# A hybrid pooling, gating and ConvFFN step, rewritten as one pass over all tokens with a list-scheduled instruction order

## Chip, cores, metric

One Trainium2 chip, all eight NeuronCores. Each core takes one of the eight prompts (2048 tokens, 16 tiles of 128) and an eighth of the samples (128 tokens, one tile), and runs all four layers by itself. The metric is device time in microseconds of the slowest core. A program on all eight cores has a second, slower state in some of its executions, in which the cores of one die (sometimes of both) have a lower granted TensorE clock: 0.808 to 0.816 on die 0 and 0.891 to 0.911 on die 1 in one of the kernel before (3957 us). Each run is marked fast or slow, and only fast runs are compared.

## The reference, cut to what matters

```python
def layer(x, ...):
    z = rmsnorm(x, norm1_g) @ w_in                     # 1024 -> 1536
    p, u, v = z[..., :512], gelu(z[..., 512:1024]), rmsnorm(gelu(z[..., 1024:]), v_norm_g)
    a = pool_mixer(p, pool_past, ...)                  # trailing mean minus token, 4 maps of 128x128, scale
    s = spatial_gate(u, v, w_spatial, b_spatial)       # u * (causal 128x128 W_s @ v + b)
    x = x + concatenate([a, s]) @ w_out                # 1024 -> 1024
    h = rmsnorm(x, norm2_g)
    g = h @ w_gate                                     # 1024 -> 2816
    conv = conv_b + sum(conv_w[k] * shifted(g, k) for k in range(3))
    return x + (gelu(conv) * (h @ w_up)) @ w_down, ...
```

A prompt starts with empty pasts; a sample tile starts from 15 past pooling rows and 2 past gate rows for each sequence. The last rows of both kinds are outputs too.

## The kernel before

It makes two passes ("halves") of all four layers: 8 prompt tiles and the sample tile, then the other 8 prompt tiles. Each pass reads all weights. The FFN goes in groups of 2 chunks of 128 columns. No scheduler reorders it: each engine gets its instructions in the order in which the program names them.

```python
halves = [([8 prompt tiles] + [sample tile], [("p", [0,1,2,3]), ("p", [4,5,6,7]), ("s", [8])]),
          ([8 prompt tiles],                 [("p", [0,1,2,3]), ("p", [4,5,6,7])])]
for half, (tiles, subtiles) in enumerate(halves):
    for l in range(L):
        mixer_phase(half, l, tiles)                 # tile by tile, software-pipelined by hand
        ...
        ffn_phase(half, l, subtiles, hook)
# ... in ffn_phase, for each group of G = 2 chunks, each set of tiles, each chunk:
pg.op("pe", gu, ...)                                # gate and up, 8 + 8 matmuls of 512 columns
if is_s:                                            # sample tile: state in and out by PE transposes
    e.transpose(ps[ga][:, 256:288], scs[csi][:, ci * 128:(ci + 1) * 128], identf[0:32, 0:32])
    # ... later: ACT copies the tail out, PE transposes it, ACT copies it to cso
if want_cs:                                         # last set of the second half: 2 rows, element by element
    pg.dma("sp", ..., [(ncp_o[l][:, c * 128:(c + 1) * 128].rearrange("r p -> p r"), gst[:, 512:514])], slow=True)
# ... down projection of the group, then
pg.op("dve", lambda e: e.tensor_tensor(out=xs[:, slot, :], in0=psall[...], in1=xs[:, slot, :], op=ALU.add))
# cuts: tables, norms, pooling bands, pool map (4 matmuls and 4 scalings a tile), state outputs
```

## Time and profile before

| | before |
|---|---|
| time, median of 20 runs | 3760.6 us (3691.3 to 3899.8) |
| profiled execution, slowest core | 3724.7 us |
| TensorE busy, and standing still | 2902 us, 823 us |
| mean granted clock, that core | 0.930 |
| VectorE, ScalarE, GpSimd busy | 2209, 1349, 465 us |

TensorE (PE) is the fullest engine, and still it stands still for a fifth of the span. "Busy" for matmuls is the time in which at least one was in flight; the granted clock has to be read beside it, since where it is recorded as 0.5 the 512-column matmuls start every 0.43 us (at 317 us of this trace) in place of 0.215 (at 600 us, clock 1.0). PSUM is `psall` in the lines; all 16736 matmuls of this trace write it. The lines themselves are in the prediction.

### The profile page before, as it was taken

The page shows a single profiled execution, that of the slowest core. Times are in us where ns is not written, and L with a number is a line of the kernel's source. Part 1 is how long each engine was busy: PE and PEld are TensorE (multiplying, and loading weights), DVE is VectorE, ACT ScalarE, POOL GpSimd, SP SyncE. Part 2 cuts the span into 40 slices and gives each one's busy share as a digit, 9 for nine tenths or more (in the row PEclk, how much of TensorE's full clock was granted, in tenths as well). Part 3 has the DMA queues.
Part 4 walks back from the last instruction along what each step waited for, and adds up shares of the span by engine and source line. Part 5 has one row for each costly group of instructions (what it writes and reads, how often), then busy time and mean ns, then how long its engine had stood idle before and what let it go on. Part 6 is the DMA issues. An engine that isn't in the chain of part 4 may idle for free.

```text
span 3724.7 us, 50015 instructions; the slowest of 8 cores (3643.9 to 3724.7 us)
## 1 busy us (share of the span) xinstructions
PE 2901.6 (78%) x16736; PEld 1424.5 (38%) x16736; DVE 2209.0 (59%) x2839; ACT 1348.5 (36%) x2883; POOL 465.4 (12%) x851
## 2 busy tenths in 40 slices
PE   0778887788887888878884768887687766887887
PEld 0434444444343444534432423353233422344333
DVE  0457775577745777457773456755475445664667
ACT  0433334333343333533343423353233422344333
POOL 1210002100021000210002210021000200011000
PEclk9999999999999999999997989998798988999998
DMA  9043230432304332043323399708986199940983
GB/s 182 13 94 66 54 58 14 100 67 54 59 13 100 67 57 56 12 95 66 63 45 119 38 86 79 64 9 82 81 57 50 9 85 69 63 47 7 60 60 79
DMA packets 105794, 230.92 MB, mean 62 GB/s; under 512 B 34700, under 2 KB 40012, under 8 KB 105480
## 3 DMA queue, kind: packets, MB, share of 16 engines
q0 software_dynamic: 58832, 183.20, 43.0%
q1 hardware_dynamic: 46712, 44.53, 5.6%
q8 instruction: 140, 2.29, 0.3%
q14 instruction: 110, 0.90, 0.1%
HBM read 398.19 MB, written 13.58 MB: 111 GB/s over the span
## 4 chain that ended last, share of the span: by engine, by line
PE 33%; DMA 22%; DVE 22%; issue 11%; ACT 8%; SPq 2%; another core or an unknown queue 1%; POOL 1%; DVEq 1%; ACTq 0%; POOLq 0%
DMA ncp<-sb_S 15%; DVE sb_xs L719 8%; PE psall L619 7%; PE psall L622 6%; DMA sb_wsl<-wgu_h 4%; PE psall L541 4%; DVE sb_S L686 3%; PE psall L542 3%; DVE sb_S L683 3%; PE psall L713 3%; PE psall L715 3%; PE psall L429 3%; DVE sb_H L516 2%; PE psall L430 2%; ACT sb_S L696 2%
## 5 line engine op out<-in xcount | busy, mean ns | idle before, releaser
L719 DVE TENSOR_TENSOR sb_xs<-psall,sb_xs 128x1024 f32<-128x1024 f32 x748 | 883.3, 1218 | 241.5 <-PE psall L715 236.0
L619 PE MATMUL psall<-sb_h2T,sb_wsl 128*128 128x512 bf16 (+1 forms) x3520 | 768.6, 364 | 292.2 <-DVE sb_H L698 168.2
L622 PE MATMUL psall<-sb_h2T,sb_wsl 128*128 128x512 bf16 (+1 forms) x3520 | 740.4, 355 | 0.0
L696 ACT ACTIVATE sb_S<-sb_S 128x512 f32<-128x512 f32 (+1 forms) x440 | 248.8, 565 | 1141.3 <-DVE sb_S L686 970.1
L713 PE MATMUL psall<-sb_wdl,sb_H 128*128 128x512 bf16 x1496 | 588.1, 393 | 32.3 <-DVE sb_xs L719 28.0
L715 PE MATMUL psall<-sb_wdl,sb_H 128*128 128x512 bf16 x1496 | 587.3, 393 | 0.0
L619 PEld LDWEIGHTS psall<-sb_h2T,sb_wsl 128*128 128x128 bf16 x3520 | 315.8, 101 | 680.7 <-issue 411.6
L698 DVE TENSOR_TENSOR sb_H<-sb_S,psall 128x512 bf16<-128x512 f32 (+1 forms) x440 | 267.4, 608 | 348.8 <-ACT sb_S L696 317.0
L622 PEld LDWEIGHTS psall<-sb_h2T,sb_wsl 128*128 128x128 bf16 x3520 | 329.9, 101 | 350.0 <-issue 31.8
L683 DVE SCALAR_TENSOR_TENSOR sb_S<-sb_S,sb_cw 128x512 f32<-128x512 f32 x352 | 262.3, 745 | 234.0 <-ACT sb_S L680 230.9
L108 POOL DMA_DIRECT2D sb_wsl<-wgu_h x176 | 94.7, 543 | 2227.2 <-PE psall L622 2196.1
L669 ACT ACTIVATE sb_S<-psall 128x512 f32<-128x512 f32 x352 | 207.7, 590 | 407.1 <-PE psall L622 239.4
L686 DVE SCALAR_TENSOR_TENSOR sb_S<-sb_S,sb_cw 128x512 f32<-128x512 f32 x352 | 264.4, 751 | 38.4 <-DVE sb_S L683 2.3
L680 ACT ACTIVATE sb_S<-psall,sb_cb,sb_cw 128x512 f32<-128x512 f32 x352 | 268.0, 761 | 0.0
L541 PE MATMUL psall<-sb_wo,sb_H 128*128 128x512 bf16 x544 | 217.1, 399 | 56.2 <-DVE sb_H L516 50.0
L407 PE MATMUL psall<-sb_identb,sb_H 128*128 128x128 bf16 x1088 | 83.9, 232 | 226.5 <-DVE sb_H L400 226.5
L340 POOL TENSOR_TENSOR sb_stats<-sb_stats,sb_cconst 128x1 f32<-128x1 f32 x221 | 122.8, 556 | 963.9 <-ACT sb_JK L337 679.2
L713 PEld LDWEIGHTS psall<-sb_wdl,sb_H 128*128 128x128 bf16 x1496 | 150.5, 101 | 230.7 <-issue 84.8
L429 PE MATMUL psall<-sb_wi,sb_H 128*128 128x512 bf16 x544 | 217.1, 399 | 17.7 <-ACT sb_JK L337 11.4
L545 DVE TENSOR_TENSOR sb_xs<-psall,sb_xs 128x1024 f32<-128x1024 f32 x68 | 83.3, 1225 | 233.0 <-PE psall L542 225.9
L542 PE MATMUL psall<-sb_wo,sb_H 128*128 128x512 bf16 x544 | 216.6, 398 | 0.0
L430 PE MATMUL psall<-sb_wi,sb_H 128*128 128x512 bf16 x544 | 216.5, 398 | 0.0
(91 smaller groups left out, 2519.1 us busy)
## 6 DMA issues: line engine op xcount, KB each, us to landing
sb_wsl<-wgu_h POOLq DMA_DIRECT2D x176, 512.0 KB, 9.8
sb_wdl<-wd_h POOLq DMA_DIRECT2D x88, 512.0 KB, 13.7
sb_wi<-wi_h POOLq DMA_DIRECT2D x64, 384.0 KB, 17.2
sb_wo<-wo_h POOLq DMA_DIRECT2D x64, 256.0 KB, 24.8
sb_xs<-x_all SPq DMA_DIRECT2D x17, 512.0 KB, 26.1
y_all<-sb_S SPq DMA_DIRECT2D x34, 256.0 KB, 2.6
sb_g1bc<-g SPq DMA_DIRECT2D x8, 512.0 KB, 4.8
sb_g2bc<-g SPq DMA_DIRECT2D x8, 512.0 KB, 12.6
```

The costliest lines, as they stand in the source:

```text
L429: e.matmul(ps[1][:], lhsT=hT[:, k, :], rhs=wi[:, k, 0:512], start=(k == 0), stop=(k == KD - 1))
L430: ins = e.matmul(ps[2][:], lhsT=hT[:, k, :], rhs=wi[:, k, 1024:1536], start=(k == 0), stop=(k == KD - 1))
L541: e.matmul(ps[4][:], lhsT=mixT[:, k, :], rhs=wo[:, k, 0:512], start=(k == 0), stop=(k == KD - 1))
L542: ins = e.matmul(ps[5][:], lhsT=mixT[:, k, :], rhs=wo[:, k, 512:1024], start=(k == 0), stop=(k == KD - 1))
L619: e.matmul(ps[ga][:, 0:ntok], lhsT=wg_[:, k, ci * 128:(ci + 1) * 128], rhs=h2T[:, k, col0:col0 + ntok], start=(k == 0), stop=(k == KD - 1))
L622: ins = e.matmul(ps[gb][:, uo:uo + ntok], lhsT=wu_[:, k, ci * 128:(ci + 1) * 128], rhs=h2T[:, k, col0:col0 + ntok], start=(k == 0), stop=( ...
L683: pg.op("dve", lambda e, acc=acc, gst=gst, w1=w1: e.scalar_tensor_tensor(out=acc[:, 0:512], in0=gst[:, 1:513], scalar=w1, in1=acc[:, 0:512 ...
L686: pg.op("dve", lambda e, acc=acc, gst=gst, w0=w0: e.scalar_tensor_tensor(out=acc[:, 0:512], in0=gst[:, 0:512], scalar=w0, in1=acc[:, 0:512 ...
L696: pg.op("act", lambda e, acc=acc, ge=ge, ntok=ntok: e.activation(out=ge[:, 0:ntok], in_=acc[:, 0:ntok], func=AF.Gelu), reads=[accB], write ...
L713: e.matmul(ps[ya][:], lhsT=hh[:, ci, li * 128:(li + 1) * 128], rhs=wd_[:, ci, 0:512], start=(ci == 0), stop=(ci == gn - 1))
L715: ins = e.matmul(ps[yb][:], lhsT=hh[:, ci, li * 128:(li + 1) * 128], rhs=wd_[:, ci, 512:1024], start=(ci == 0), stop=(ci == gn - 1))
L719: pg.op("dve", lambda e, slot=slot, ya=ya: e.tensor_tensor(out=xs[:, slot, :], in0=psall[:, ya * 512:(ya + 2) * 512], in1=xs[:, slot, :], ...
```

## The change

One pass: all 17 tiles' residual (17 x 4 KB a partition) stays in SBUF, and every weight is read once. Each layer is a first sweep (input projection, pooling bands, spatial gate), a fold of the pool map into the first half of w_out, a second sweep (output projection, residual, norm, transpose) and an FFN in groups of 4 or 3 chunks. States are laid out so that they need no transposes and are stored in one transfer. The program builds a graph of operations with modelled durations, and a list scheduler sets the order on each engine.

```diff
-G = 2
+GROUPS = [4, 4, 4, 4, 3, 3]
...
+    def schedule(self):                 # earliest start first; among the ready, lowest program index
+        ...
+            if avail[e]:
+                o = ops[heapq.heappop(avail[e])]
+            else:
+                o = ops[heapq.heappop(wait[e])[1]]
...
+        xs = SB("xs", (128, NT, D), F32)             # NT = 17
+        wsl = [SB(f"w{i}", (128, 3072), BF16) for i in range(NSLOT)]     # 9 slots, one ring for all weights
...
+        def fold_pool(l):
+            for g in range(4):
+                    e.matmul(ps[b], lhsT=pw[:, g, :], rhs=wov(l, g, 0, 512), start=True, stop=True)
+                    ...
+                pg.op("act", ..., out=wov(l, g, 0, 1024), in_=psall[:, b * 512:(b + 2) * 512])
...
+                    if smp:                          # first sweep, sample tile, after the last use of w_in
+                        for i in range(4):
+                            used("wi", l, i)         # sends the loads that take over these slots
+                    ...
+                        spast = tmp[:, 2 * BLK:3 * BLK].bitcast(BF16)[:, 0:1024]...
+                        pg.dma("pool", "spast", [(spast[0:120], sp_d[l].rearrange("(a r) c -> r a c", a=2))], ...)
...
+            sets = [(list(range(4 * i, 4 * i + 4)), False) for i in range(4)] + [([SMP], True)]
+                        pg.op("pool", 0.4, lambda e: e.tensor_copy(out=halo, in_=src), ...)   # conv rows, was on ACT
...
+        for l in range(L):
+            sweep1(l)
+            fold_pool(l)
+            sweep2(l)
+            ...
+            ffn(l)
+        pg.schedule()
+        pg.emit()
```

## The prediction

> **What bounds the kernel now.** I read the page's engine totals first, then the granted clock of all cores, the table of waits of TensorE, the groups by line and form, the DMA issues, and the order of instructions around single gaps.
>
> ```profile
> span 3724.7 us, 50015 instructions; the slowest of 8 cores (3643.9 to 3724.7 us)
> PE 2901.6 (78%) x16736; PEld 1424.5 (38%) x16736; DVE 2209.0 (59%) x2839; ACT 1348.5 (36%) x2883; POOL 465.4 (12%) x851
> core 1: 3724.7 us, clock 0.930
> ```
>
> No other engine is near full, so TensorE sets the end, but badly: it stands still for 3725 - 2902 = 823 us and its mean granted clock is 0.93. What would it need if it never waited? The order of instructions gives the pace at full clock: successive 512-column matmuls of line 541 and 542 start at 599.90, 600.12 and 600.34, so 0.215 us each (the 0.38 us printed is a pipelined duration); a run of 32 128-column ones of line 464 takes 1.95 us, 0.056 us each. By form the kernel has 10800 of 512 columns (4 x 1408 gate and up, 2 x 1496 down, 4 x 544 projections) and 5760 of 128, plus 176 small fp32 transposes (some 35 us): 2322 + 323 + 35 = 2680 us. The rest of the 2902 busy us, some 220, is lost clock (2680 / 0.93 = 2882). The order around 315 us shows how it is lost:
>
> ```profile
> 314.89 0.27 PE L663 MATMUL psall<-sb_identf_s,sb_csl 128*32 128x128 f32 x1 [2.01 <-ACT sb_csl L660]
> ...
> 316.90 0.63 PE L713 MATMUL psall<-sb_wdl,sb_H 128*128 128x512 bf16 x1
> ...
> 318.61 0.45 PE L713 MATMUL psall<-sb_wdl,sb_H 128*128 128x512 bf16 x1
> 318.90 0.38 PE L715 MATMUL psall<-sb_wdl,sb_H 128*128 128x512 bf16 x1
> ```
>
> After a gap of 2.0 us the same matmul shows 0.63 us instead of 0.38, at half the pace, until full clock is back.[...] The waits name the gaps:
>
> ```profile
> PE psall L407 <- DVE sb_H L400: 226.5, 24, 98.7
> PE psall L619 <- DVE sb_H L698: 168.2, 70, 27.3
> PE psall L619 <- DMA sb_wsl<-wgu_h: 121.7, 13, 17.4
> PE psall L663 <- ACT sb_csl L660: 104.4, 63, 2.4
> ACT sb_S L669 <- DMA ncp<-sb_S: 167.6, 30, 28.6
> ```
>
> The columns are total, times, longest. (a) 98.7 us: the start, in which sixteen projection pieces, three FFN groups, tables and x come in before the first matmul. (b) The chain 669 to 698 waits on the transfer of the two last gate rows, up to 28.6 us each, and the matmuls of line 619 behind it; the same time has the late weight loads. This is in the second half alone, whose 8 tiles take as long (1950 to 3725) as the first half's 9 tiles. (c) 104 us: the sample tile's state transposes, a TensorE to ScalarE to TensorE ping-pong inside the in-order FFN. (d) The rest is the mixer's tile-by-tile dependences. The DMA issues say why (b) is slow:
>
> ```profile
> DMA packets 105794, 230.92 MB, mean 62 GB/s; under 512 B 34700, under 2 KB 40012, under 8 KB 105480
> ncp<-sb_S SPq DMA_DIRECT2D x88, 1.0 KB, 20.1
> ```
>
> One KB takes 20 us, because it is written as single fp32 elements; 512 KB of weights take 9.8.
>
> [...]from 2290 to 2310 us all four cores of die 1 have TensorE 19.95, 20.00, 20.00 and 20.00 of 20 us busy at 1.00. But the six times of the kernel fall into two groups, 3702 to 3720 and 3767 to 3795[...]. [...] Line 340's addition on one column takes 190 ns in the median and 1286 at worst[...].
>
> **The change, part by part.**
> *TensorE work* hardly changes. 512 columns: 10800 + 32 for folding the pool map into w_out = 10832, 2329 us. The u projection goes over tile pairs, 1024 of 256 columns at 0.108 (estimate, between the two paces) instead of 2048 of 128: 111 us. 128 columns: 128 for the sample's u, 1088 transposes, 1408 sample FFN, 560 bands, 272 spatial = 3456, 194 us; the 272 pool-map and 176 state-transpose matmuls go. Sum 2634 us: only 46 us under the 2680. The gain can come only from gaps and clock.
> *VectorE* gets lighter. Six FFN groups over 17 tiles are 408 residual additions per run instead of 748, 1.18 us each: 401 us off. The pool scaling (256 x 0.35 = 90) goes too. New sum from the old rows: conv and gate 352 x (0.745 + 0.751 + 0.688) = 769, sample 86, residual 482 + 83, norms 174, v norm 54, spatial 93, final and tables 33: 1774 us, 67% of 2634. It can't bound.
> *ScalarE*: 352 x (0.590 + 0.761 + 0.629) = 697, sample 90, squares 190, transposed copies 139, mixer 215, fold 16: 1350 us, as before; the two-column copies of lines 678 and 690 (89 us) go to GpSimd.
> *GpSimd*: 880 such copies (some 0.4 us, from line 340's 0.19 to 1.29) = 350, norm roots 442 x 0.56 = 249, some 220 DMA issues at 0.55 = 121: 720 us. Nearly all beside TensorE.
> *DMA*: weights once instead of twice. The software queue's 183 MB took 43% of the span; it becomes some 92 MB, 21%. A chunk's 0.79 MB needs about 7 us at that rate and feeds 22 us of matmuls. The single-element transfers are replaced by one contiguous store per layer. So (b), 122 + most of 168 us and its clock, disappears.
> *Start*: x (8.9 MB), g1 and four w_in pieces (3.1 MB as bf16) come first on two queues. The old start moved 18 MB in 95 us. The v-norm table stands behind all x tiles on its queue, so I expect 10 + 4 MB before it, 75 us, with three or four tiles' projections (20 us) done by then: 55 us lost instead of 99.
> *New waits.* In the second sweep the output projection and the transposes draw alternately from one ring of two PSUM pairs, so the projection always gets the same pair and waits for the residual addition: 1.22 us plus two hops, less a 0.46 us transpose, 1.3 us x 68 = 88. FFN matmuls of the first tile set fill part; I keep 35. FFN: 3% of 1930 = 58 for the gate chain of six steps (about 5 us against some 7 us of bank ring). First sweep 5% of 406 = 20. Layer boundaries, where temporary blocks change owner and the sample set's short chain comes last: 8 us x 4 = 32. End: last norm and store, 10. Half clock after the remaining longer gaps: 20.
> Sum for a fast run: 2634 + 55 + 35 + 58 + 20 + 32 + 10 + 20 = **2864 us**, TensorE at some 93% and its mean clock 0.98 or more.
>
> **The rivals.** (i) *The clock becomes the bound*[...]. For: [...]the two groups of times. Against: the dense stretch at 1.00 above.[...] (ii) *The schedule doesn't hold on the chip*: the order on every engine is fixed from modelled durations, and the loads, roots and two-column copies share GpSimd in order, so one late slot release holds copies behind it. For: before, GpSimd waited 2196 us at its weight loads[...]. Against: the copies are wanted late, and a late TensorE leaves the others slack. It would cost 5% more, 3000 us. (iii) *Nearly perfect overlap*: the list order hides sweep, boundaries and sample set: 2634 + 55 + 60 = 2750. (iv) *DMA stays the bound*: weights still read as fp32 and a chunk released only after all 17 tiles. Against: 21% share, nine slots. I give it 3%.
>
> **Range and chances.** Half for something near the sum, a quarter for the clock in some runs, so that the median of several runs lies a little over the fast sum; the rest for (ii) and (iii) about evenly. Predicted 2880 us, 2760 to 3080 eight times in ten. Nothing but (i) in full, with (ii), comes within 10% of the old time: faster 0.98, same 0.01, slower 0.01.
>
> **What will show it.** Right: TensorE busy some 2650 to 2750 us over 92% of the span, clock 0.97 or higher, VectorE near 1770, no wait of TensorE on a weight load after the start, packets under 512 B nearly gone, first matmuls by 50 us. Wrong: [...]TensorE waiting on VectorE in the FFN with VectorE waiting on GpSimd (ii); over 80 us of waits at the output projection for the residual addition (the ring). If VectorE or ScalarE durations grow under denser use, the sum is too low.

## The result, and the profile after

The changed kernel takes **2948.6 us** in the median of 10 runs (2945.3 to 3436.3); the kernel before 3760.6 us in the median of 20. Seven of the ten are fast, 2945.3 to 2950.2. The ratio of the fast runs is 0.794 (95% interval 0.791 to 0.797). Ratios are the mean time of one kernel's fast runs over that of the other's of the same rounds, so not quite the ratio of these medians. The time lies in the range, 69 us above the point of 2880 and 85 above the sum for a fast run, 2864.

The head of the page after, with the slices of TensorE and of its clock (each digit a fortieth of the span), and the DMA queues:

```profile
span 2948.3 us, 44336 instructions; the slowest of 8 cores (2934.7 to 2948.3 us)
PE 2661.4 (90%) x15038; PEld 1353.5 (46%) x15312; DVE 1716.2 (58%) x2192; ACT 1225.9 (42%) x2191; POOL 500.3 (17%) x1550
PE   2759999999995999999998699999999699999996
PEclk8879999999997999999999899999999799999998
DMA packets 44615, 127.30 MB, mean 43 GB/s; under 512 B 6700, under 2 KB 9452, under 8 KB 44328
q0 software_dynamic: 32768, 93.40, 19.6%
```

Three things are to be seen. The PE row is nines except at the start and in four single slices, one in each layer, and the clock dips in the same slices. Packets under 512 B fell from 34700 to 6700. The software queue, which carries the weights, fell from 43.0% to 19.6% of the DMA engines' time. (274 matmul records are missing in this trace, 15038 of 15312.)

Of the 3724.7 - 2948.3 = 776 us, 536 are standing still (823 to 287) and 241 busy time (2902 to 2661). With the missing records it is rather 554 and 218: a later trace of the same kernel (run after_again), with all records, has TensorE 2684 us busy and 269 standing still. The clock records of the traces, laid over the matmuls, say how much of the busy time was at half clock (0.5): 302 us before, some 50 after (48 to 51 over the cores), so 151 us lost before and 25 after. Of the 218 us of busy time, then, some 126 are clock regained and 46, by the prediction's count, work that is gone; the rest I can't place. By far the larger part of the gain is the 554 us of standing still. These are two 50 us windows of the changed kernel, with busy times and counts of PE, weight loads, VectorE, ScalarE, GpSimd, then clock, DMA share and GB/s:

```profile
900.00:950.00 50.00, 19.42 (x87) 8.35 (x90) 10.69 (x15) 7.71 (x11) 4.12 (x9) 0.63 0.54 85
1100.00:1150.00 50.00, 49.74 (x228) 22.64 (x232) 32.53 (x40) 18.81 (x31) 6.47 (x25) 1.00 0.29 47
```

In the FFN (the second) TensorE is 99% busy at full clock. From 900 to 950, between the sweeps, it is 39% busy at 0.63. The waits of TensorE name the cause (total, times, longest):

```profile
PE psall L546 <- DMA sb_tmp<-sp: 80.9, 4, 21.5
PE psall L591 <- DVE sb_tmp L530: 58.8, 5, 40.1
PE psall L409 <- DVE sb_xn L401: 34.5, 16, 13.7
PE psall L720 <- DVE sb_tmp L696: 21.6, 16, 1.7
PE psall L618 <- DVE sb_xs L627: 13.4, 16, 1.5
```

The first is the sample tile's pool state, once a layer, about 20 us each time. Of the second and third, 40.1 and 28.6 us fall into the first 110 us, the start; behind the 40.1 stand the tables (line 530 itself waits 39.2 us there for the transfer of `bsS`). Here is the state's wait in the second layer, in order of time (start, duration, engine, line; TensorE and GpSimd lines picked out):

```profile
895.19 4.30 POOL L90 DMA_DIRECT2D sb_w<-wf  x8 [3.51 <-PE psall L591]
...
899.58 0.81 POOL L90 DMA_DIRECT2D sb_tmp<-sp  x1
...
923.87 0.27 PE L546 MATMUL psall<-sb_bands,sb_tmp 128*128 128x128 bf16 x1 [21.30 <-DMA sb_tmp<-sp]
...
926.63 0.63 PE L445 MATMUL psall<-sb_w,sb_pw 128*128 128x512 bf16 x1
...
936.84 0.38 PE L618 MATMUL psall<-sb_w,sb_hT 128*128 128x512 bf16 x1
```

GpSimd sends eight weight transfers (four FFN chunks, 3.1 MB as bf16) at 895, as soon as w_in's slots are free, and the 240 KB of state behind them at 899.6; they land at 923.8. Nothing else runs: TensorE's order is fixed, and in it the fold and the second sweep come after the sample tile's bands; the fold's first matmul then waits for a bank that ScalarE empties after them (0.94 us). Then the fold (line 445) and most of the first output projection run at half clock (0.63 us), until 936.8. The landing times tell the same, before and then after:

```profile
sb_spast<-sp POOLq DMA_DIRECT2D x4, 240.0 KB, 5.0
```

```profile
sb_tmp<-sp POOLq DMA_DIRECT2D x4, 240.0 KB, 24.1
```

**The slow state.** The slow runs of the changed kernel took 3050.6, 3054.1, 3235.0 and 3436.3 us (one of them an execution that was profiled and taken again). In the last, die 1 had clocks of 0.812, 0.811, 0.808 and 0.808 and spans of 3415 to 3435 us, while die 0 had 0.966 and 2940 to 2945. In the other three die 1 had 0.867 to 0.872 (3235.0 us) and 0.926 to 0.933 (3050.6 and 3054.1), with die 0 at 0.965 to 0.967 again. No slow run of this kernel was traced, so what lowers the clock was not shown. The load alone does not: in the seven fast runs all eight cores had 0.965 to 0.967 with the same work.

### The profile page after: what moved, and what is told of

Read it like the earlier page. It is cut to its first block, busy times and chain, and to the rows that moved or that the text cites. A ratio compares the mean times of both kernels' runs of the same rounds, so it can differ in the third digit from the quotient of the medians.

```text
span 2948.3 us, 44336 instructions; the slowest of 8 cores (2934.7 to 2948.3 us)
## 1 busy us (share of the span) xinstructions
PE 2661.4 (90%) x15038; PEld 1353.5 (46%) x15312; DVE 1716.2 (58%) x2192; ACT 1225.9 (42%) x2191; POOL 500.3 (17%) x1550
## 3 DMA queue, kind: packets, MB, share of 16 engines
q0 software_dynamic: 32768, 93.40, 19.6%
## 4 chain that ended last, share of the span: by engine, by line
PE 81%; DVE 4%; DMA 4%; ACT 3%; issue 3%; SPq 2%; POOL 1%; DVEq 0%; ACTq 0%; POOLq 0%
PE psall L659 39%; PE psall L720 21%; PE psall L477 4%; PE psall L516 4%; PE psall L499 4%; PE psall L620 4%; PE psall L618 3%; DMA sb_tmp<-sp 3%; SPq L90 2%; PE psall L409 2%; DVE sb_tmp L696 1%; DVE sb_tmp L693 1%; ACT sb_xn L397 1%; DMA sb_bsS<-bsS 1%; DVE sb_xn L401 1%
## 5 line engine op out<-in xcount | busy, mean ns | idle before, releaser
L659 PE MATMUL psall<-sb_hT,sb_w 128*128 128x512 bf16 (+1 forms) x6908 | 1338.9, 346 | 19.1 <-DVE sb_tmp L703 9.4
L659 PEld LDWEIGHTS psall<-sb_hT,sb_w 128*128 128x128 bf16 x7040 | 632.4, 98 | 681.6 <-issue 13.7
L720 PE MATMUL psall<-sb_w,sb_tmp 128*128 128x512 bf16 x2926 | 676.8, 380 | 34.7 <-DVE sb_tmp L696 21.6
L725 DVE TENSOR_TENSOR sb_xs<-psall,sb_xs 128x1024 f32<-128x1024 f32 x408 | 498.7, 1222 | 164.2 <-PE psall L720 161.0
L693 DVE SCALAR_TENSOR_TENSOR sb_tmp<-sb_tmp,sb_cw 128x512 f32<-128x512 f32 (+1 forms) x440 | 292.7, 670 | 294.0 <-ACT sb_tmp L691 281.5
L720 PEld LDWEIGHTS psall<-sb_w,sb_tmp 128*128 128x128 bf16 x2992 | 290.5, 98 | 373.6 <-issue 47.3
L703 DVE TENSOR_TENSOR sb_tmp<-sb_tmp,psall 128x512 bf16<-128x512 f32 (+1 forms) x440 | 263.1, 603 | 238.5 <-ACT sb_tmp L701 197.1
L701 ACT ACTIVATE sb_tmp<-sb_tmp 128x512 f32<-128x512 f32 (+1 forms) x440 | 246.1, 562 | 341.4 <-DVE sb_tmp L696 339.2
L691 ACT ACTIVATE sb_tmp<-psall,sb_cb,sb_cw 128x512 f32<-128x512 f32 (+1 forms) x440 | 312.1, 709 | 7.0 <-DVE sb_tmp L703 6.7
L696 DVE SCALAR_TENSOR_TENSOR sb_tmp<-sb_tmp,sb_cw 128x512 f32<-128x512 f32 (+1 forms) x440 | 293.6, 668 | 26.0 <-DVE sb_tmp L693 0.9
L620 PE MATMUL psall<-sb_w,sb_hT 128*128 128x512 bf16 x544 | 211.3, 388 | 5.5 <-DVE sb_xs L627 3.2
L618 PE MATMUL psall<-sb_w,sb_hT 128*128 128x512 bf16 x508 | 196.9, 388 | 19.1 <-DVE sb_xs L627 13.4
L516 PE MATMUL psall<-sb_w,sb_hT 128*128 128x512 bf16 x539 | 127.7, 379 | 0.9 <-issue 0.6
```

What stands on the lines that cost most here:

```text
L516: ins = e.matmul(ps[b], lhsT=hT[:, k, t * 128:(t + 1) * 128], rhs=wiv(l, k, 1024, 1536), start=(k == 0), stop=(k == KD - 1))
L618: e.matmul(ps[b], lhsT=hT[:, k, t * 128:(t + 1) * 128], rhs=wov(l, k, 0, 512), start=(k == 0), stop=(k == KD - 1))
L620: ins = e.matmul(ps[b + 1], lhsT=hT[:, k, t * 128:(t + 1) * 128], rhs=wov(l, k, 512, 1024), start=(k == 0), stop=(k == KD - 1))
L659: ins = e.matmul(ps[b][:, 0:ntok], lhsT=w[:, o + k * 128:o + (k + 1) * 128], rhs=hT[:, k, col:col + ntok], start=(k == 0), stop=(k == KD - 1))
L691: pg.op("act", t_act(ntok, 2), lambda e, a3=a3, p3=p3, w2=w2, bia=bia: e.activation(out=a3, in_=p3, func=AF.Identity, scale=w2, bias=bia), ...
L693: pg.op("dve", t_dve(ntok, True), lambda e, a3=a3, v1=v1, w1=w1: e.scalar_tensor_tensor(out=a3, in0=v1, scalar=w1, in1=a3, op0=ALU.mult, o ...
```

## The experiments

The theory after the result: (1) the remaining loss is one transfer's place in a queue, plus the start; (2) the gain came from the order and from state transfers, and the lower DMA volume, the larger groups and the fold gave little by themselves. All kernels ran correctly. The changed kernel's fast runs lie between 2945 and 2955 us on the chips on which it ran; the kernel before differs more from chip to chip (3691 to 3870 in fast runs), so absolute times of the variants are compared with 2945 to 2955, and ratios to the kernel before are given where they matter.

### Is it the queue? The weights held back

```diff
-                    if smp:
-                        for i in range(4):
-                            used("wi", l, i)
...                     # after the state's load:
+                        for i in range(4):
+                            used("wi", l, i, [tB[2][0]])     # gate/up halves wait for the state
```

> The changed kernel with one order turned round: in each layer the four FFN chunk loads (eight transfers) that take over the slots of w_in are held until the sample tile's pool state has landed; the state load keeps its place in the program and its buffer. Theory Q (the state waits in the software DMA queue behind 3.1 MB of weights): the state lands some 5 us after its issue, as it did in the kernel before (5.0 us in the median), TensorE's wait for it falls from 80.9 us to under 12 us in four layers, the half clock after it goes, and the time falls by 80 to 110 us, to 2840 to 2870. Rival B (the buffer is handed over too late, or this 120-partition load is itself slow): the wait stays at 15 us or more a layer and the time within 1%.

Measured: 2893.8 to 2895.5 us in fast runs, some 55 us off: between the theories. The wait of TensorE, and the order in the second layer:

```profile
PE psall L545 <- DMA sb_tmp<-sp: 31.6, 4, 9.3
```

```profile
884.07 2.19 POOL L90 DMA_DIRECT2D sb_w<-wf  x4 [3.52 <-PE psall L590]
886.37 0.81 POOL L90 DMA_DIRECT2D sb_tmp<-sp  x1
888.76 0.58 PE L590 MATMUL psall<-sb_wsS,sb_tmp 128*128 128x128 bf16 x4 [2.57 <-DVE sb_tmp L527]
897.77 0.27 PE L545 MATMUL psall<-sb_bands,sb_tmp 128*128 128x128 bf16 x1 [8.43 <-DMA sb_tmp<-sp]
```

My edit was not complete: it held the gate/up halves of the chunks, and the down halves (256 KB each) were still free, so all four of them went ahead. With these four, 1 MB, ahead of it in place of eight and 3.1 MB, the state landed 11 us after its issue and not 24. So what stands ahead in the queue is the cause; with nothing ahead and the old 5.0 us, it would have landed at about 892, some 3 us after TensorE ran dry. That last step is an estimate, not run: the SyncE queue moved some 1 MB of its own between 883 and 892, and what this adds was not measured.

### Is it the whole of it? The state early, in another buffer

```diff
+                if q == 8:
+                    ix = ring("xn", 2)
+                    spast, spB = xn[ix][:].rearrange("p (a c) -> p a c", a=2), xnB[ix]
+                    pg.dma("pool", "spast", [(spast[0:120], ...)], 491520, writes=[spB])
...
-                        spast = tmp[:, 2 * BLK:3 * BLK]...
-                        pg.dma("pool", "spast", ..., writes=tB[2])
```

(With it goes one more change: the sample's normalised v rows are written only after an explicit wait for all that the write depends on, VectorE's own earlier work included. The program-order and the last kernel have it too.)

> The changed kernel with the pool state loaded into one of the two buffers of normalised x, which are free in the first sweep, so that it waits neither for a tile's spatial gate nor behind the weight loads. Theory Q and rival B both expect the wait of 80.9 us to vanish; the time falls by 90 to 120 us, to 2830 to 2860, mean clock from 0.965 to about 0.985. If it falls by less than the 81 us, other work (fold, second sweep) was waiting there anyway and the gap was not the state's alone.

Measured: 2865.7 to 2866.7 us in the four fast runs, some 85 us off, a little less than expected; TensorE 94% busy, clock 0.979. The wait is gone: the transfer was taken off the path. Against the complete trace of the changed kernel the standing still fell by 83 us (269 to 186) and the busy time by 4 only (2684 to 2680). So the gap came back in full, and the half clock did not, because the fold's chain stays where it was: TensorE still waits at the fold (lines 444 and 621: 22.5 us in all, 22.0 before) and runs it at half clock (0.63 us in place of 0.38, in the second layer).

### What is one reading of the weights worth?

```diff
+    scr = nc.dram_tensor("scr", [L * 29, 128, 3072], BF16).ap()
...
+                pg.dma("pool", "scr", [(scr[n][:, 0:m], src)], 512 * m, out=True)     # after each weight load
```

> The changed kernel with every weight load followed by a second one of the same size into a scratch tensor in HBM: the weight traffic of two passes, to see what reading the weights once is worth here. If DMA is hidden: the software queue's share doubles from 19.6% to about 40%, the FFN keeps its pace with no wait on a weight load, and only the pool state, which sits in the same queue, lands later: its wait goes from 20 to 40 or 50 us a layer, 80 to 130 us more in all (3030 to 3080). Rival (DMA volume matters by itself): TensorE waits for FFN weights as in the kernel before (over 100 us) and the time grows by over 200 us.

Measured: 3692 us, as if the rival were right. But the experiment was badly made. The scratch loads depended on nothing, so the list scheduler sent all 116 of them in the first 100 us; the DMA engines were full for some 900 us, and two waits took nearly all of it: one for the tables at the start grew to 95 us, and that for the state in the first layer to 683:

```profile
DMA  9999999999222223130322111303222112122202
```

```profile
PE psall L550 <- DMA sb_tmp<-sp: 743.2, 4, 682.6
```

It shows how far one transfer behind others in this queue can stretch, and nothing about a second pass. The repeat tied each scratch load to the releases of the real load before it:

```diff
+                real = pg.ops[-1]
+                o = pg.dma("pool", "scr", [(scr[n][:, 0:m], src)], 512 * m, out=True)   # rows padded to 3088
+                o.deps = list(real.deps)
```

> As a_double, but every scratch load is tied to the same releases as the real load that it follows, so that the doubled weight traffic is spread over the run as a second pass would spread it (in a_double the scheduler was free to send all 116 scratch loads in the first 100 us). If DMA is hidden: FFN at full pace without waits for weights, the pool state behind twice as much in its queue, its wait up from 20 to about 40 us a layer: 2949 + 80 to 130 = 3030 to 3080. Rival (volume matters by itself): waits of TensorE on FFN weights over 100 us in all, time over 3150.

Measured: 3104.6 to 3108.7 us in fast runs, 5.3% more than the changed kernel, somewhat above the expected range. All waits of TensorE on a DMA, and the queue:

```profile
PE psall L552 <- DMA sb_tmp<-sp: 189.9, 4, 50.2
PE psall L483 <- DMA sb_w<-wi: 25.3, 1, 25.3
```

```profile
q0 software_dynamic: 49472, 183.59, 43.6%
```

At 43.6%, the share of the kernel before, TensorE does not wait once for an FFN weight; the state's wait grew by 109 us, as the queue theory wants, and the waits of the start by some 45. The FFN takes 554 us a layer in both traces, from its first matmul to its last. So reading the weights once is worth about 5% here, and all of it at two places where one transfer stands behind others: the start, and the state. The volume as such is hidden. (The doubled loads go to HBM and not to SBUF, so this imitates a second pass and is not one.)

### What is the list order worth?

```diff
-        self.order = order
+        self.order = {e: [o for o in ops if o.eng == e] for e in self.ENG}
```

> The changed kernel with every engine running its instructions in the order in which the program names them, no list schedule. My theory: TensorE then waits for the gate chain (about 5 us) before each set's down projection, 96 sets: 480 us; for the spatial gate of every tile (4 us, 68 tiles): 270; for the norm before every transpose in the second sweep (5 us, 68): 340; for the sample chunks: 200; and half clock after many of these. 3900 to 4500 us, slower than the kernel before. Rival: buffers and sets alone do it and the order is worth little: under 3100.

Measured: 5034 and 5048 us in the two fast runs (ratio to the kernel before 1.314), more than expected. The profiled execution fell in the slow state (clock 0.75), so its times are upper values, but the waits can be ranked:

```profile
PE psall L409 <- DVE sb_xn L401: 771.6, 136, 88.6
PE psall L721 <- DVE sb_tmp L704: 392.9, 120, 5.4
PE psall L592 <- DVE sb_tmp L530: 205.9, 64, 3.5
```

They are the waits I named (norm before the transposes, gate chain before the down projection, v norm before the spatial gate). I had 340 us for the first, for the second sweep alone; it comes 136 times, in the last FFN group too. Without its order the rewritten kernel is 31% slower than the kernel before: the program as written names its steps chain by chain, and only a reordering makes the rest possible. Whether one by hand would do as well was not tried.

### What are groups of four worth?

```diff
-GROUPS = [4, 4, 4, 4, 3, 3]
+GROUPS = [2] * 11
```

> The changed kernel with FFN groups of 2 chunks as before, so 748 residual additions in place of 408. VectorE's sum grows by 340 x 1.22 = 415 us to some 2130; in the FFN it becomes about as long as TensorE (465 against 482 us a layer). Theory: TensorE stays the bound with VectorE's additions on the path of the two down-projection bank pairs, 2 to 8% slower, 3010 to 3180. Rival: VectorE had slack, within 1%.

Measured: 2986.7 to 2988.2 us in fast runs, 1.1 to 1.3% more: less than my theory, more than the rival. The 340 additions are there (748 in place of 408, VectorE's busy time 2070 us in place of 1716), and what TensorE waits for them is this, with the output projection's line below:

```profile
PE psall L720 <- DVE sb_xs L725: 19.3, 23, 2.4
PE psall L618 <- DVE sb_xs L627: 28.5, 36, 1.5
```

Of 354 us of added VectorE work some 20 reach the FFN's path (TensorE stands still for 63 us there, in place of 41 in the complete trace of the changed kernel), and some 13 more line 618 of the second sweep (28.5 in place of 15.7). (The changed kernel itself was not run on this chip, so the percentage rests on its times on two others, which agree within 0.3%.)

### What is the fold worth?

```diff
-            fold_pool(l)
...                     # per tile: 4 matmuls of pw on the pooled rows, then
+                        pg.op("dve", ..., e.tensor_scalar(out=mixA[:, g, :], in0=ps[b][...], scalar1=psc[...], ...))
```

> The changed kernel with the pool map applied to every tile again (4 matmuls of 128 columns, 4 VectorE scalings) and not folded into w_out. TensorE +15 us for the map, -7 us for the fold; VectorE +272 x 0.35 = 95 us, in a sweep where it has half its time free; the fold's chain on ScalarE between the sweeps (some 8 us a layer) goes. Theory: within 1% of the changed kernel, 2930 to 2975. If the fold is an important part, slower by over 2%.

Measured: 2939.6 us in the one fast run of five (clock 0.970 and over on all cores); the other four had one die or both in the slow state, 3083 to 3399. In the fast run it is 0.3% less than the changed kernel, inside the expected range. One fast run is enough to say that the fold is no important part; which of the two is better it can't say.

### The state stores, alone, in the kernel before

```diff
-   pg.dma("sp", ..., [(ncp_o[l][:, c * 128:(c + 1) * 128].rearrange("r p -> p r"), gst[:, 512:514])], slow=True)
+   pg.op("act", lambda e: e.activation(out=gtl[:, c, :], in_=gst[:, 512:514], func=AF.Copy), ...)
+   if c == NCH - 1:
+       pg.dma("sp", "o_cp", [(ncp_o[l], gtl[:].rearrange("p c r -> p (c r)"))], ...)
```

> The kernel before with one thing of the change: the last two gate rows are gathered in one tile and stored once a layer in one contiguous transfer, in place of 88 transfers of single elements. My account of the kernel before expects: no wait on that store, no late weights in the second half, packets under 512 B down by some 22,000, the second half (8 tiles) about 1560 us in place of 1775, and the time down by 180 to 280 us (5 to 7.5%), to 3450 to 3560. If the second half is slow for another reason, the time changes by under 2%.

Measured: 3484.6 to 3491.3 us; ratio of the fast runs to the kernel before on the same chip 0.925 (0.918 to 0.931). The second half is dense now, and most of the small packets are gone. First the PE slices and the software queue of the kernel before, where the slices behind the gap in the middle fall to 6 and 7:

```profile
PE   0778887788887888878884768887687766887887
q0 software_dynamic: 58832, 183.20, 43.0%
```

Then those with the one store a layer:

```profile
PE   0778887788888788877888488997899879987997
DMA packets 82433, 230.91 MB, mean 66 GB/s; under 512 B 11340, under 2 KB 16652, under 8 KB 82120
q0 software_dynamic: 58832, 183.20, 30.0%
```

The same 183 MB of weights cost 30.0% of the DMA engines in place of 43.0%: the element-wise stores had slowed the weight transfers (512 KB for gate and up land in 6.8 us in the median without them, 9.8 with them). Each of the 88 stores of 1 KB took 20.1 us in the median; the one of 22 KB a layer takes 4.1. 88 KB of output, badly laid out, were worth 7.5%, over a third of the whole gain of the change.

### The start, and four repairs together

```diff
         load_w(4)
+        load_consts()
+        layer_tables(0)
         for t in range(2, NT):
             load_x(t)
-        load_consts()
-        layer_tables(0)
```

Baseline, on the same chip:

> The changed kernel itself on the chip of the next two, as their baseline: 2945 to 2951 us in fast runs, 3050 to 3440 where one die is in the slow state.

Measured: 2951.9 to 2954.9 us, all four fast; a little over the expected range, which had come from another chip.

> The changed kernel with only the order of the first loads changed: constants and layer tables before x tiles 2 to 16 on the SyncE queue. If the tables behind 7.5 MB of x hold the first sweep (TensorE waits 40 us for the first v norm), that wait goes and 20 to 35 us are won, 2915 to 2930. Rival: w_in and x are the bound of the start, the wait moves to x and under 10 us are won.

Measured: 2926.2 to 2929.8 us in fast runs, 25 us (0.8%) less than the baseline. The wait of 40 us on the tables is gone, and the wait for the first norms rose:

```profile
PE psall L409 <- DVE sb_xn L401: 54.5, 16, 28.1
```

It was 35.5 us in the baseline: about half of what the tables had cost moved to x, so both are part of the start.

The last kernel puts together the early state, this start, `fold_pool(l)` called in the first sweep at the seventh tile pair, and the sample set third of five (`sets.insert(3, ([SMP], True))`) in each FFN group.

> Four repairs of the changed kernel together: pool state early into a buffer of normalised x (82 us measured), tables before x (20 to 35), the pool map folded in the middle of the first sweep instead of after it (5 to 10), the sample tile third and not last in each FFN group, so that its chain of short steps is covered by a full set at the end (10 to 20). Sum 117 to 147 us off 2948: 2800 to 2830 in fast runs, TensorE busy 95%, mean clock 0.985. If fold and sample order give nothing: 2835 to 2845.

Measured: **2789.2 to 2790.8 us** in the three fast runs, 5.5% less than the changed kernel on the same chip (0.727 against 0.769 of the kernel before), better than the expected range; three runs were slow, 2884, 3187 and 3231. Head and waits:

```profile
span 2788.9 us, 44582 instructions; the slowest of 8 cores (2782.5 to 2788.9 us)
PE 2664.1 (96%) x15312; PEld 1349.7 (48%) x15312; DVE 1713.5 (61%) x2192; ACT 1224.2 (44%) x2191; POOL 501.7 (18%) x1550
PEclk9999999999999999999999999999999999999998
```

```profile
PE psall L409 <- DVE sb_xn L401: 61.7, 19, 28.9
PE psall L727 <- DVE sb_tmp L710: 17.4, 13, 3.2
```

With no gap of over 3.2 us after the start the clock is 0.995 or more on every core. State and start had been worth 85 and 25 us by themselves; the other 50 or so are left for the fold's and the sample set's new places, and for the clock that comes back when no gap is left. No run separates them, but the traces say roughly where they lie. Compared with the early state alone, TensorE stands still some 8 us less in each stretch between the FFNs of two layers (7 in place of 15), 9 us less inside the four FFNs (33 in place of 41), and is busy 15 us less (2664 in place of 2680), at a mean clock of 0.995 in place of 0.979.

## Why the prediction was right, and where it was off

The direction, the mechanism and the range held: TensorE's work stayed, its gaps and half clock went, no other engine came near, and the stores of single elements were a large part. By its terms:

| term of the prediction | said | showed |
|---|---|---|
| TensorE at full clock | 2634 us | about 2664 (busy time of the last kernel, all records, clock 0.995) |
| VectorE, ScalarE | 1774, 1350 us | 1716, 1226 |
| GpSimd | 720 us (copies at 0.4) | 500 (copies at 0.21 to 0.22) |
| software DMA queue | 21% | 19.6% |
| start | 55 us | 72 (40.1 + 28.6 + 3.2) |
| pool state's load | not named | 81 |
| half clock after longer gaps | 20 | some 20 (busy 2684 in the complete trace of the changed kernel, against 2664) |
| second sweep's PSUM ring | 35 | 17 (lines 618 and 620 on 627: 13.4 + 3.2) |
| FFN stalls | 58 | some 45 (lines 720 and 659), 13 of them in the last 60 us |
| first sweep | 20 | 19 (line 591 without the start's 40) |
| layer boundaries | 32 | 22 (the fold's chain: 7.4 + 5.7 + 5.1 + 3.8) |
| end, after the last matmul | 10 | 11 |

**What was missing** is in the step "New waits": I looked for waits at PSUM rings, chains and block owners, and judged DMA by its share ("a chunk needs about 7 us and feeds 22 us of matmuls"), so the transfers seemed hidden. The state's load is not a weight, and it is asked for late, in a block that the last pair of prompt tiles gives back, behind the loads that w_in's last use sends. Program text shows it: `used("wi", ...)` stands ahead of the state's transfer. Together with 17 us at the start this is 98 us; the smaller errors in the other terms nearly cancel (TensorE +30, FFN, ring and boundaries -41). "No wait of TensorE on a weight load after the start" held. That one of a small transfer *behind* weight loads should be asked for too, I had not thought of.

**The clock.** I said 0.98 or more and it was 0.965, for the same reason: four gaps of 17 to 21.5 us, each with half clock after it (8 to 11 us of busy time at 0.5). Without them, the gap of the start and the fold's chain it is 0.995. For the same reason TensorE is busy 90 to 91% of the span and not 92. I also misread what the clock had cost before. The mean clock is taken over the whole span, idle time too (527 us of the 3725 were at 0.5, which makes 0.929), so 2680 / 0.93 = 2882 is no check of the busy time: of the 2902 us, 302 were at half clock, which makes 151 us lost and not some 220. Nor did half clock follow every gap: in the trace of the kernel before, whose clock records begin at 107 us, it began in the gap or within 3.5 us of its end for 24 of the 47 gaps of 1.8 to 2.2 us, and for all 42 of 3 us or more. And where it followed, a long gap was not paid again in full: after the gap of 2.0 us some 2 us were lost (half clock for 3.4 us), after one of 21 us some 5, and 25 us in the whole changed kernel, beside 269 of standing still.

**Three smaller readings.** The second half of the kernel before is not as long as the first: 1775 us for 8 tiles against 1950 for 9, of which 99 are the start, so 222 us a tile against 206. That 1 KB takes 20.1 us as single elements, and 22 KB in one contiguous store 4.1 (run b_ncp), shows that single-element stores are slow; why they are, no run shows. The spread of line 340 on GpSimd goes with what VectorE does beside it: of its 221 executions all 88 of over 400 ns (up to 1286) overlap a VectorE multiplication with two SBUF inputs (lines 400 and 751), the 14 that overlap the residual addition of line 719, which has one input in PSUM, and no such multiplication take 184 to 191 ns, and the 105 that overlap nothing on VectorE 179 to 195.

**The rivals.** (i) is real in some runs (3051 to 3436 us, with mean clocks of 0.808 to 0.933 on die 1), and not in the median. (ii) was wrong: GpSimd's copies were short and the fixed order held. (iii) was nearly what the last kernel reached, 2790 against 2750. (iv) was wrong for the FFN, which not even doubled traffic made wait; the same traffic at the start and before the state cost 5%.

**Where the gain came from** I had right in kind, but the parts named in the change are not equal. Shown by single edits: the state stores 7.5% in the kernel before; one reading of the weights 5%; groups of four 1.1 to 1.3%; the fold nothing that one fast run can show; and the list order is the condition of the rest, since without it the new program is 31% slower than the old. These can't be added up: some were measured from the old side and some from the new. The state transposes that went (104 us of waits in the kernel before, (c) of the prediction) have no run of their own.

## What to carry to other kernels

Ask of every small transfer which large ones stand ahead of it in its queue when it is issued, and who waits for it; a DMA share of 20% says nothing about that (at 19.6% the 240 KB of state landed 24.1 us after their issue), and the remedy is to issue it early into a buffer that is free by then. Where TensorE is the bound and its work can't shrink, count the gaps, and add what half clock takes after them: here some 2 us after a gap of 2 us where it followed (24 of 47), so that such a gap is paid nearly twice, but only some 5 after one of 21. When a scheduler orders your instructions, give an experiment's extra work the dependences that it would have in earnest, or the scheduler will move it to where it tests something else.

## What the runs showed of the hardware

- The slow state is a state of some runs, not of the load alone. In three of the six runs of the last kernel all eight cores had a mean clock of 0.995 or more over 2.8 ms, and in the fast runs of the changed kernel 0.964 to 0.967. Where it came, the mean clock of the slow die lay between 0.808 (changed kernel, 3436 us) and 0.958 (last kernel, 2884 us).
- Back to back at full clock, 512-column matmuls start every 0.215 us and 128-column ones every 0.056 us, each with its own weight load (kernel before, at 600 and 607 us; 16736 matmuls, 16736 weight loads).
- A gap of 2.0 us, right after dense matmuls, could be enough for half clock (0.63 us in place of 0.38, at 315 us of the kernel before); it followed on 24 of the 47 gaps of 1.8 to 2.2 us after 107 us. Coming back took 5.0 us of nearly dense matmuls (one pause of 0.22 us) at 932 us of the changed kernel.
- The time from issue to landing grew with what stood ahead in the queue: 240 KB took 5.0 us in the kernel before, and in the changed one and its variants 10.7 behind four transfers, 24.1 behind eight, 50.4 with doubled traffic (medians of the four layers).
